# The low parts of the xBC weights are formed on GpSimd

## The chip, the core and the metric

The kernel runs on one core of one Trainium2 chip. Its time is the device time of one execution in microseconds (us), the median of several runs. Five engines work beside each other, each through its own queue in order: TensorE (PE: matmuls and transposes), VectorE (DVE), ScalarE (ACT), GpSimd (POOL) and SyncE (SP), which issues nearly all DMAs.

## The reference

One decoder layer on 1024 tokens of width 1024. What matters here is the mixer: one input projection gives q, k, v, a gate z, xBC and dt. Group A is attention with a window of 128 over 8 heads, group B a state-space scan in chunks of 128:

```
h = rmsnorm(x, norm1) * (1 + scale1) + shift1
proj = h @ w_in                              # -> q | k | v | z | xBC | dt
y_attn = rmsnorm(sliding_window_attention(q, k, v, sinks, rel_bias))
xbc = silu(conv4(xBC) + conv_b)              # depthwise, 1024 channels -> xs, B, C
y_ssm = rmsnorm((ssd_scan(xs, dt, A, B, C) + D_skip * xs) * silu(z))
x = x + gate1 * (concat(y_attn, y_ssm) @ w_o)
x = x + gate2 * swiglu(rmsnorm(x, norm2) * (1 + scale2) + shift2)
out = rmsnorm(x, final_norm)
```

All in float32.

## The kernel before

Every large product is made of three matmuls on split operands: a high part, rounded to the format fp32r, and a low part, the rest. `mm3` (L93 to L96) adds high x high (L94), high x low (L95) and low x high (L96). A weight tile is split by `split`: ScalarE casts the raw tile to the high part (L90), VectorE subtracts it from the raw tile (L81, called from L91). `load_w` (L205) takes a raw buffer from a ring of three, loads it by a DMA on SP's queue and splits it into one of three slots for high and low parts. A raw buffer is free once both its cast and its subtraction have read it; SP issues its DMAs in program order, so a load that waits for a buffer also holds what is behind it.

The stages around the change: q and k projections, then v, z and dt (`vz_tile`), then from about 156 us attention tiles 0 to 3 (`attn`), the xBC projection and convolution of the first half of the sequence (`xbc_tile(0, f)`, f = 0 to 7), between them rows of the modulation weights through the same raw ring (`ada_row`, L409 on VectorE), scan chunks 0 to 3 (`ssd_chunk`), attention tiles 4 to 7 and `xbc_tile(1, f)`; then the output projection from 316 us, the second norm at 394 us, the scan chunks 4 to 7 beside the first SwiGLU columns, and SwiGLU up to the end.

`xbc_tile` multiplies one 1024 x 128 tile of weights by 512 tokens: 24 matmuls into the bank psx. Three of the 16 tiles are loaded ahead (`xw`); the other 13 call `load_w` here (L503). ScalarE copies the bank (L508) and makes the first conv step (L513), VectorE the other three (L515), then ScalarE a tanh (L517) and VectorE the product (L518).

The chain of an attention tile: scores on TensorE (pss, L459), bias and maximum on VectorE (L463, eight), a small subtraction (L81, 128x8), exponentials on ScalarE (L467, L469), transposes on TensorE (pst, L479), copies on ScalarE, the product with v (psy, L486), scaling on VectorE (L84), squares on ScalarE (L490), one column on VectorE (L145), its power on GpSimd (L146), scaling on ScalarE (L492), transposes on TensorE (psm_a, L438). That of a scan chunk: seg (L581), decay on ScalarE, cb and its causal product (L591), three products on VectorE (L84), the skip product on GpSimd (L603), the state's decay on GpSimd (L625), ydg and st on TensorE (L613, L621), sums on VectorE (L87), squares on ScalarE (L629), L145, the power L146, scaling (L632), transposes (psm_s, L438).

The order of instructions on each engine is laid down when the program is built, by a scheduler that places every instruction by its own estimate of when its inputs will be ready; each engine then keeps that order on the chip.

Of the kernel before, what the change touches and what calls it, by code (L numbers as in the profile page):

```python
# [7 lines left out]
F32 = mybir.dt.float32  # L8
F32R = mybir.dt.float32r
AF = mybir.ActivationFunctionType  # L10
ALU = mybir.AluOpType
# [4 lines left out]
P = 128  # L16
D = 1024
KT = 8
# [20 lines left out]
def hymba_layer(ctx: ExitStack, tc: tile.TileContext, x, ada01, ada_rest, w_qk, w_vz, w_xbc,  # L39
                w_o, w_gu, w_dn, prm, bc, rel, adab_g, fnorm, cst, out):  # L40
    nc = tc.nc
# [29 lines left out]
    def dma(out, in_):  # L71
        tc.keep_in_program_order(nc.sync.dma_start(out, in_))

    def mm_bank(name):
        return PS.tile([P, 512], F32, tag="mm", bufs=4, name=name)
# [4 lines left out]
    def sub(out, a, b):  # L80
        nc.vector.tensor_tensor(out=out, in0=a, in1=b, op=ALU.subtract)  # L81
# [7 lines left out]
    def split(h, l, raw):  # L89
        nc.scalar.copy(h, raw)  # L90
        sub(l, raw, h.bitcast(F32))  # L91
# [102 lines left out]
    def wtiles(shape):  # L194
        n = 1
        for d in shape:
            n *= d
        raw = raw_ring(shape)
        hl = ws_ring([2, n])
        h, l = hl[:, 0], hl[:, 1]  # L200
        if len(shape) == 2:
            h, l = (v.rearrange("p (a b) -> p a b", a=shape[0]) for v in (h, l))
        return raw, h, l

    def load_w(src, shape):  # L205
        raw, h, l = wtiles(shape)
        dma(raw, src)
        split(h, l, raw)
        return h, l

    def ada_load(sec, kt, ring_):
# [131 lines left out]
    for kt in range(KT):  # L343
        raw = raw_ring([648])
        dma(raw, w_vz[kt])
        w2 = view(WV, 1296 / 256 * (kt - 3), [2, 648]) if kt >= 3 else view(FR, 64 + 5.0625 * kt, [2, 648])
        h, l = w2[:, 0], w2[:, 1]
# [25 lines left out]
    def fm_tile(half, h, l, bank, kts=range(KT)):  # L373
        for kt in kts:
            mm3(bank, h[:, kt], l[:, kt], hts[half][kt][:, 0], hts[half][kt][:, 1], kt == 0, kt == KT - 1)
# [45 lines left out]
    dma(brow, adab_g[0:1])  # L421
    add(arow[0:1], arow[0:1], brow)
    xw = [load_w(w_xbc[f], [KT, P]) for f in range(3)]
    for t in range(4, 8):
        vz_tile(t)
# [74 lines left out]
              [view(FA, 56.03125 + 2 * f, [512]) for f in range(4)] + [view(FA, 46, [512]), view(FB, 18, [512]), view(FB, 20, [512]), view(FA, 64.03125, [512])]]  # L500

    def xbc_tile(half, f):
        h, l = xw[f] if half == 0 and f < len(xw) else load_w(w_xbc[f], [KT, P])  # L503
        ps = mm_bank(f"psx{half}_{f}")
        fm_tile(half, h, l, ps)
        rw = xraw_ring([515])
        nc.vector.tensor_copy(rw[:, 0:3], halo[:, f])
        nc.scalar.copy(rw[:, 3:515], ps)  # L508
        if half == 0:
            nc.vector.tensor_copy(halo[:, f], rw[:, 512:515])  # L510
        y = xbc_sb[half][f]
        cw = lambda k: pt[:, C_CW + 8 * k + f:C_CW + 8 * k + f + 1]
        nc.scalar.activation(y, ps, AF.Identity, scale=cw(3), bias=pt[:, C_CB + f:C_CB + f + 1])  # L513
        for k in range(3):
            nc.vector.scalar_tensor_tensor(out=y, in0=rw[:, k:k + 512], scalar=cw(k), in1=y, op0=ALU.mult, op1=ALU.add)  # L515
        th = th_ring([512])
        nc.scalar.activation(th, y, AF.Tanh, scale=0.5)  # L517
        nc.vector.scalar_tensor_tensor(out=y, in0=th, scalar=1.0, in1=y, op0=ALU.add, op1=ALU.mult)  # L518
# [133 lines left out]
    for f in range(8):  # L652
        xbc_tile(0, f)
        for _ in range(MOD_ROWS[f]):
            sec, kk = rows.pop(0)
            ada_row(sec, [view(FB, 18, [D])] if sec == 3 else mod2[1], [kk])
# [6 lines left out]
    for f in range(8):  # L663
        xbc_tile(1, f)
# [60 lines left out]
    def gate_up(f, half, out, then=None):  # L725
        pss = []
        for s in range(2):
            if (f, s) not in resident:
                resident[(f, s)] = load_w(w_gu[f + NF * s], [KT, P])
            h, l = resident[(f, s)]  # L730
            ps = mm_bank(f"psgu{f}{s}{half}")
            for kt in range(KT):
                t = h2[half][kt]
                mm3(ps, h[:, kt], l[:, kt], t[:, 0], t[:, 1], kt == 0, kt == KT - 1)
            pss.append(ps)
            if then:
                then(s)
        nc.scalar.activation(out, pss[0], AF.Silu)
        mul(out, out, pss[1])
# [182 lines left out]
    for i in range(NP):  # L922
        a = pair_ring([4, 512])
        for r in range(2):
            f = 2 * i + r
# [230 lines left out]
```

## Time and profile before

| | |
|---|---|
| median of 3 runs | 1148.93 us (1146.12 to 1150.82) |
| the profiled execution | 1144.76 us, span 1143.0 us |
| PE busy | 1105.0 us, 97% of the span |
| DVE busy | 842.6 us, 74% |
| ACT busy | 517.2 us, 45% |
| POOL busy | 244.6 us, 21%, 185 instructions |

Busy shares are means over stages with different limits, so the stretch around the change is read by itself. PE's busy time is modelled at the end of each matmul. Spans on POOL are rough. A row's last part in square brackets is the idle time of the engine ahead of it and what ended that.

### The profile page before, as it was taken

How to read it: one execution, taken by the hardware profiler on the slowest of the kernel's cores; microseconds unless marked ns; L12 is line 12 of the kernel's file. 1: busy time of each engine (PE TensorE's matmuls, PEld its weight loads, DVE VectorE, ACT ScalarE, POOL GpSimd, SP SyncE). 2: the span in 40 equal slices, each digit the busy share in tenths (PEclk: the TensorE clock that was granted, in tenths of full speed). 3: DMA queues.
4: the chain of work that ended last, by engine and by line, in shares of the span. 5: the costliest groups of instructions: out<-in, count | busy, mean ns of one | idle time of the engine just before them, and what ended most of it. 6: DMA issues, size and time to landing. Idle time of an engine off the chain costs nothing. (4 is left out here: it accounts for less than half of the span.)

```text
span 1143.0 us, 15497 instructions
## 1 busy us (share of the span) xinstructions
PE 1105.0 (97%) x5376; PEld 912.4 (80%) x5376; DVE 842.6 (74%) x1490; ACT 517.2 (45%) x1007; POOL 244.6 (21%) x185
## 2 busy tenths in 40 slices
PE   7999999999999889999999999999999999999996
PEld 6788987787788668887888888888888878888875
DVE  6895368788856466546888888898788648787856
ACT  4573256756565456535443333333333325555431
POOL 0100000001200111000222124554445010451352
PEclk9999999999999969999999999999999999999998
DMA  7555644421320253236753247556764468788733
GB/s 267 189 173 174 238 151 145 137 74 38 148 75 19 102 185 119 76 127 221 249 189 125 67 148 263 194 179 217 256 201 160 157 226 306 252 292 281 234 104 147
DMA packets 80449, 197.29 MB, mean 173 GB/s; under 512 B 9154, under 2 KB 10226, under 8 KB 80244
## 3 DMA queue, kind: packets, MB, share of 16 engines
q1 hardware_dynamic: 74164, 184.95, 47.4%
q10 hardware_dynamic: 6208, 11.37, 2.8%
q8 instruction: 42, 0.69, 0.2%
q14 instruction: 35, 0.29, 0.1%
HBM read 149.87 MB, written 47.98 MB: 173 GB/s over the span
## 5 line engine op out<-in xcount | busy, mean ns | idle before, releaser
L81 DVE TENSOR_TENSOR FR<-FP,FR 128x512 fp32r<-128x512 f32 (+4 forms) x244 | 195.0, 822 | 68.8 <-ACT FR L90 68.3
L90 ACT CAST FR<-FP 128x512 fp32r<-128x512 f32 (+3 forms) x236 | 157.7, 682 | 185.6 <-PE psg L95 79.8
L797 POOL TENSOR_TENSOR GF<-GF 128x512 f32<-128x512 f32 x77 | 124.0, 1633 | 68.9 <-DMA GF<-in_w_dn 65.8
L94 PE MATMUL psg<-FR 128*128 128x512 f32 x306 | 119.0, 389 | 0.0
L95 PE MATMUL psg<-FR 128*128 128x512 f32 x306 | 119.0, 389 | 0.0
L96 PE MATMUL psg<-FR 128*128 128x512 f32 x306 | 119.0, 389 | 0.0
L146 POOL TENSOR_TENSOR FP<-FP 128x1 f32<-128x1 f32 (+1 forms) x40 | 28.3, 713 | 407.8 <-DVE FP L145 351.6
L87 DVE TENSOR_TENSOR GF<-GF,psg 128x512 f32<-128x512 f32 x126 | 84.2, 680 | 30.4 <-PE psg L96 27.9
L90 ACT CAST FR<-GF 128x512 fp32r<-128x512 f32 x77 | 47.4, 619 | 79.8 <-PE psg L95 54.5
L94 PE MATMUL psg<-GR,FR 128*128 128x512 f32 x198 | 77.0, 389 | 0.0
L95 PE MATMUL psg<-GR,FR 128*128 128x512 f32 x198 | 77.0, 389 | 0.0
L96 PE MATMUL psg<-GR,FR 128*128 128x512 f32 x198 | 77.0, 389 | 0.0
L81 DVE TENSOR_TENSOR FR<-GF,FR 128x512 fp32r<-128x512 f32 x77 | 73.1, 951 | 0.9 <-ACT FR L90 0.7
L95 PEld LDWEIGHTS psg<-FR 128*128 128x128 f32 x306 | 57.4, 188 | 12.0
L94 PEld LDWEIGHTS psg<-FR 128*128 128x128 f32 x306 | 57.4, 188 | 11.9
L96 PEld LDWEIGHTS psg<-FR 128*128 128x128 f32 x306 | 57.4, 188 | 11.9
L803 POOL TENSOR_TENSOR GD<-GD 128x512 f32<-128x512 f32 x23 | 35.7, 1562 | 119.7 <-ACT GD L415 57.7
L800 POOL TENSOR_TENSOR GF<-GF 128x512 f32<-128x512 f32 x11 | 15.5, 1405 | 194.3 <-DVE GF L84 156.2
L94 PE MATMUL psgu<-FR 128*128 128x512 f32 x128 | 51.6, 407 | 2.5 <-DVE FR L179 1.3
L94 PE MATMUL psx<-FR 128*128 128x512 f32 x128 | 52.2, 408 | 0.0
L96 PE MATMUL psgu<-FR 128*128 128x512 f32 x128 | 51.4, 403 | 0.5 <-DVE FR L81 0.5
L95 PE MATMUL psx<-FR 128*128 128x512 f32 x128 | 51.8, 405 | 0.0
(318 smaller groups left out, 2748.6 us busy)
## 6 DMA issues: line engine op xcount, KB each, us to landing
FP<-in_w_gu SPq DMA_DIRECT2D x52, 512.0 KB, 4.2
FP<-in_ada_rest SPq DMA_DIRECT2D x24, 512.0 KB, 4.4
actds<-GF SPq DMA_DIRECT2D x44, 256.0 KB, 2.7
GF<-in_w_dn SPq DMA_DIRECT2D x22, 512.0 KB, 4.6
wdndt<-GF SPq DMA_DIRECT2D x44, 256.0 KB, 4.4
FP<-actds SPq DMA_DIRECT2D x44, 256.0 KB, 4.4
FP<-wdndt SPq DMA_DIRECT2D x44, 256.0 KB, 4.4
FP<-actda SPq DMA_DIRECT2D x33, 256.0 KB, 4.2
```

The costliest lines, as they stand in the source:

```text
L81: nc.vector.tensor_tensor(out=out, in0=a, in1=b, op=ALU.subtract)
L87: nc.vector.tensor_tensor(out=out, in0=a, in1=b, op=ALU.add)
L90: nc.scalar.copy(h, raw)
L94: nc.tensor.matmul(ps, lhsT=lh, rhs=rh, start=first, stop=False)
L95: nc.tensor.matmul(ps, lhsT=lh, rhs=rl, start=False, stop=False)
L96: nc.tensor.matmul(ps, lhsT=ll, rhs=rh, start=False, stop=last)
L146: nc.gpsimd.tensor_tensor(out=r, in0=r, in1=mhalf[:, 0:count], op=ALU.pow)
L797: nc.gpsimd.tensor_tensor(out=out, in0=a, in1=b, op=ALU.subtract)
L800: nc.gpsimd.tensor_tensor(out=out, in0=a, in1=b, op=ALU.add)
L803: nc.gpsimd.tensor_tensor(out=out, in0=a, in1=b, op=ALU.mult)
```

## The change

`load_w` gets a parameter for the engine that forms the low part; without it VectorE does, as before. The 13 calls from `xbc_tile` name GpSimd. The cast stays on ScalarE. Lines behind `load_w` move down by one, and in the changed kernel the cast and subtraction of `load_w` are L208 and L209.

```
-    def load_w(src, shape):
+    def load_w(src, shape, low=None):
         raw, h, l = wtiles(shape)
         dma(raw, src)
-        split(h, l, raw)
+        nc.scalar.copy(h, raw)
+        (low or nc.vector).tensor_tensor(out=l, in0=raw, in1=h.bitcast(F32), op=ALU.subtract)
         return h, l
...
     def xbc_tile(half, f):
-        h, l = xw[f] if half == 0 and f < len(xw) else load_w(w_xbc[f], [KT, P])
+        h, l = xw[f] if half == 0 and f < len(xw) else load_w(w_xbc[f], [KT, P], nc.gpsimd)
```

The scheduler then lays the engines out anew from the fourth xBC tile to the middle of the first output projection; SP's order is the same.

GpSimd, from the norms of the first stage to scan chunk 1, before (L146 128x1 are powers of row norms, the last four of the twelve those of attention tiles 0 to 3):

```order
L146 TENSOR_TENSOR FP<-FP 128x1 x12
L603 TENSOR_TENSOR FB<-FB,FP 128x512
L146 TENSOR_TENSOR FP<-FP 128x2
L625 TENSOR_TENSOR FA<-FA,FP 128x512
L603 TENSOR_TENSOR FB<-FB,FP 128x512
L146 TENSOR_TENSOR FP<-FP 128x2
```

And now, in the changed kernel's line numbers:

```order
L146 TENSOR_TENSOR FP<-FP 128x1 x9
L209 TENSOR_TENSOR FR<-FP,FR 128x1024
L146 TENSOR_TENSOR FP<-FP 128x1
L209 TENSOR_TENSOR FR<-FP,FR 128x1024 x3
L146 TENSOR_TENSOR FP<-FP 128x1
L209 TENSOR_TENSOR FR<-FP,FR 128x1024 x2
L146 TENSOR_TENSOR FP<-FP 128x1
L209 TENSOR_TENSOR FR<-FP,FR 128x1024 x3
L604 TENSOR_TENSOR FB<-FB,FP 128x512
L146 TENSOR_TENSOR FP<-FP 128x2
L209 TENSOR_TENSOR FR<-FP,FR 128x1024
L626 TENSOR_TENSOR FA<-FA,FP 128x512
```

Nine of the thirteen stand between the powers of attention tile 0 and scan chunk 0; the powers of tiles 2 and 3 come behind three and two of them.

ScalarE, at the end of attention tile 1 (FR<-psm_a is the cast of its transposed output, FR<-FP 128x1024 a weight cast, L469 or L470 the exponentials of tile 2), before:

```order
L492 ACTIVATE FA<-FA,FP 128x512
L90 CAST FR<-FP 128x1024
L440 CAST FR<-psm_a_1557 128x4x128
L508 COPY FA<-psx_3_1860 128x512
L467 ACTIVATE FP<-FP 128x8
L469 ACTIVATE FB,FP<-FB,FP 128x256 x8
```

And now:

```order
L493 ACTIVATE FA<-FA,FP 128x512
L208 CAST FR<-FP 128x1024
L441 CAST FR<-psm_a_1557 128x4x128
L208 CAST FR<-FP 128x1024
L468 ACTIVATE FP<-FP 128x8
L470 ACTIVATE FB,FP<-FB,FP 128x256 x8
```

A second weight cast, the third of the thirteen, stands ahead of the exponentials, where the copy of a finished xBC bank stood; that copy is now behind them.

TensorE, at scan chunk 0 (psx_0_2709 and psx_1_2745 are the banks of xBC tiles 0 and 1 of the second half, with 24 matmuls each), before, where 19 of tile 1 are done:

```order
L96 MATMUL psx_1_2745<-FR 128x512
L94 MATMUL psx_1_2745<-FR 128x512
L581 MATMUL seg_0_2120<-FR 128x512
L581 MATMUL seg_1_2124<-FR 128x512
L587 MATMUL cb_2128<-FA 128x128 x2
```

And now:

```order
L96 MATMUL psx_0_2709<-FR 128x512
L94 MATMUL psx_1_2745<-FR 128x512
L95 MATMUL psx_1_2745<-FR 128x512
L96 MATMUL psx_1_2745<-FR 128x512
L94 MATMUL psx_1_2745<-FR 128x512
L95 MATMUL psx_1_2745<-FR 128x512
L96 MATMUL psx_1_2745<-FR 128x512
L582 MATMUL seg_0_2120<-FR 128x512
L582 MATMUL seg_1_2124<-FR 128x512
L588 MATMUL cb_2128<-FA 128x128 x2
```

Chunk 0 begins 13 matmuls earlier, after 6 of tile 1.

## Rows read from the trace of the kernel before

**Rows 1.** Windows: us, busy us (count) of PE, PEld, DVE, ACT, POOL; PEclk; DMA

```profile
156.00:236.00 80.00, 74.68 (x425) 60.27 (x423) 67.00 (x181) 54.20 (x132) 4.90 (x4) 1.00 0.45 149
236.00:316.00 80.00, 77.09 (x414) 62.23 (x413) 68.82 (x120) 46.53 (x93) 13.04 (x11) 1.00 0.25 86
316.00:394.00 78.00, 77.36 (x454) 63.41 (x452) 43.81 (x124) 45.26 (x129) 2.21 (x4) 1.00 0.14 46
394.00:420.00 26.00, 18.68 (x72) 13.89 (x73) 19.07 (x41) 12.63 (x21) 5.56 (x6) 0.66 0.57 208
```

**Rows 2.** Waits of PE, 156 to 316 us: total us, times, longest us

```profile
PE psm_a L438 <- ACT FA L492: 3.4, 4, 1.1
PE psm_s L438 <- ACT FA L632: 2.0, 3, 1.0
PE pst L479 <- ACT FB L469: 1.1, 2, 0.8
```

**Rows 3.** Lines by form, DVE, 156 to 316 us: busy us, mean ns

```profile
L81 DVE TENSOR_TENSOR FR<-FP,FR 128x1024 fp32r<-128x1024 f32 x13 | 15.8, 1214 | 0.5 <-ACT FR L90 0.5
```

**Rows 4.** Source lines L797 and L146, POOL: ns minimum/median/maximum, first and last start

```profile
L797 POOL TENSOR_TENSOR GF<-GF x77: 1275/1734/2175, 561.9 to 923.5; 128x512 f32<-128x512 f32 x77
L146 POOL TENSOR_TENSOR FP<-FP x40: 544/556/1461, 10.8 to 1137.9; 128x1 f32<-128x1 f32 x32, 128x2 f32<-128x2 f32 x8
```

**Rows 5.** Timeline of POOL and DVE near 562 us: start us, us

```profile
561.92 5.57 POOL L797 TENSOR_TENSOR GF<-GF 128x512 f32<-128x512 f32 x3
...
562.85 1.79 DVE L81 TENSOR_TENSOR FR<-GF,FR 128x512 fp32r<-128x512 f32 x1
```

**Rows 6.** Timeline of PE, ACT and DVE at attention tile 1, 175 to 178 us

```profile
175.67 0.39 PE L94 MATMUL psx<-FR 128*128 128x512 f32 x1
...
177.03 0.39 PE L94 MATMUL psx<-FR 128*128 128x512 f32 x1
...
177.94 0.44 PE L479 MATMUL pst<-FP,FB 128*128 128x128 f32 x2 [0.30 <-ACT FB L469]
...
175.09 1.05 ACT L90 CAST FR<-FP 128x1024 fp32r<-128x1024 f32 x1 [1.04 <-DMA FP<-in_w_xbc]
...
175.98 0.69 DVE L518 SCALAR_TENSOR_TENSOR FA<-FA 128x512 f32<-128x512 f32 x1
176.59 0.16 DVE L81 TENSOR_TENSOR FP<-FP 128x8 f32<-128x8 f32 x1
```

**Rows 7.** Timeline of DVE and SP before attention tile 2, 196 to 198 us

```profile
196.55 1.22 DVE L81 TENSOR_TENSOR FR<-FP,FR 128x1024 fp32r<-128x1024 f32 x1
...
197.83 0.33 SPq L72 DMA_DIRECT2D FP<-in_w_xbc  x1
```

**Rows 8.** DMA issues, 150 to 320 us: count, KB each, median us to landing

```profile
FP<-in_w_xbc SPq DMA_DIRECT2D x13, 512.0 KB, 3.8
```

**Rows 9.** Timeline of ACT, DVE and POOL at attention tile 2, 204 to 210 us

```profile
204.62 1.05 ACT L90 CAST FR<-FP 128x1024 fp32r<-128x1024 f32 x1
...
208.06 1.21 DVE L81 TENSOR_TENSOR FR<-FP,FR 128x1024 fp32r<-128x1024 f32 x1
...
208.22 1.46 POOL L146 TENSOR_TENSOR FP<-FP 128x1 f32<-128x1 f32 x1 [18.89 <-DVE FP L145]
```

**Rows 10.** Timeline of DVE at scan chunks 0 and 1, 243 to 278 us

```profile
243.55 1.21 DVE L81 TENSOR_TENSOR FR<-FP,FR 128x1024 fp32r<-128x1024 f32 x1
...
246.63 1.22 DVE L81 TENSOR_TENSOR FR<-FP,FR 128x1024 fp32r<-128x1024 f32 x1 [0.54 <-ACT FR L90]
...
248.69 1.22 DVE L84 TENSOR_TENSOR FR<-FB,FP 128x1024 fp32r<-128x1024 f32 x1
...
259.64 1.21 DVE L81 TENSOR_TENSOR FR<-FP,FR 128x1024 fp32r<-128x1024 f32 x1
...
275.58 1.22 DVE L81 TENSOR_TENSOR FR<-FP,FR 128x1024 fp32r<-128x1024 f32 x1
...
276.79 1.22 DVE L81 TENSOR_TENSOR FR<-FP,FR 128x1024 fp32r<-128x1024 f32 x1
```

## The prediction

> **What bounds the kernel now.** I read the windows first, then TensorE's waits, then the engines around each wait. The 13 moved subtractions all run between 156 and 316 us, while the two half-sequence xBC convolutions, attention tiles 0 to 3 and scan chunks 0 to 3 are interleaved. In that stretch TensorE is busy 74.68 and 77.09 us of 80 and 80 [rows 1], so 160 - 151.8 = 8.2 us are open. VectorE is busy 67.00 + 68.82 = 135.8 of 160 us (85%), ScalarE less, GpSimd 17.9 us. So TensorE's matmuls bound the stretch, and its 8.2 us of gaps come from chains on the other engines. The waits name them [rows 2]: 3.4 us before the transposes of the attention output (psm_a), 2.0 us before those of the scan output (psm_s), 1.1 us before those of the probabilities (pst). After the stretch TensorE hardly waits (77.36 of 78 us [rows 1]), so a gap made or closed in the stretch stays in the total. 8.2 us is 0.7% of the run: no relief of VectorE there can give more.
>
> **What is removed.** Thirteen instructions on VectorE of 1.214 us each, 15.8 us [rows 3].
>
> **What is added.** Thirteen subtractions of 128x1024 on GpSimd. The trace has none of that size. The nearest is the 128x512 tensor_tensor with two full SBUF inputs, 1.275 us at its shortest, 1.734 us median, 2.175 us longest; a one-column one takes 0.544 us [rows 4]. If the whole 0.544 is a fixed part, a 128x1024 takes 2 x (1.275 - 0.544) + 0.544 = 2.0 us; if nothing is fixed, 2.55 us; with contention on both halves 4.35 us. Whether a write in the rounded format (fp32r) costs GpSimd anything extra no row shows; on VectorE it does not. I take 2.4 us, near the end without a fixed part, since that row has the same operands: 13 x 2.4 = 31 us.
>
> **What GpSimd does to VectorE.** Near 562 us GpSimd runs three 128x512 in a row in 5.57 us, and VectorE's 128x512 subtraction beside them takes 1.79 us [rows 5]; a two-input 128x512 with GpSimd at rest takes 0.69 us [rows 6]. The two alternate: one runs, the other waits. It goes both ways: a one-column power on GpSimd beside one of the moved subtractions takes 1.46 us and not its usual 0.556 [rows 4, 9]. [...] How much of the 31 is felt depends on what stands next on VectorE, so I went through the places.
>
> **First attention tile, at 176 us.** The cast of the first moved tile ends at 176.14 (175.09 + 1.05); VectorE then runs a 0.69 us instruction from 175.98, and behind it stands the small subtraction that all exponentials wait for, at 176.59 [rows 6]. ScalarE's and VectorE's order here is unchanged. In the alternation seen above GpSimd's subtraction gets its turn at 176.6 and holds it until 179.0, and the small one, with two SBUF inputs, comes behind it: 2.4 us later. TensorE's wait before pst at 177.94 (now 0.30 us) grows to about 2.7. The matmul order up to here is the same in both kernels, so nothing covers it: +2.4 us. If the small one gets in first, 0.
>
> **Second tile, at 190 to 198 us.** The third cast now stands on ScalarE ahead of the exponentials. Its data cannot be there at once: SP issues that weight load only when the subtraction of the tile before frees its buffer, at 197.83 just behind 196.55 + 1.22 [rows 7]. On GpSimd that subtraction would follow its cast at 191.0 and free the buffer at 193.4; with a landing of 3.8 us [rows 8] ScalarE's queue stands until 197.2 and the exponentials begin near 198.4, some 0.9 us later than now. But TensorE's new order has 17 xBC matmuls between the scores and pst where 13 stood. One matmul comes each (177.03 - 175.67) / 6 = 0.227 us [rows 6], so four are 0.9 us: 0 in sum. The weights themselves come earlier, not later (193.4 against 197.8 us), so no matmul waits for them.
>
> **Powers behind subtractions.** GpSimd now has subtractions right ahead of the powers of tiles 2 and 3. The cast ends at 205.67 (204.62 + 1.05), a 2.4 us subtraction after at most 0.7 us of contention ends near 208.1 to 208.8, and a free power of 0.55 ends at 208.7 to 209.3; now it ends at 208.22 + 1.46 = 209.7, disturbed by the very subtraction that moves [rows 9]. Cost 0 or a little gain; the wait of TensorE behind it (the longest psm_a wait, 1.1 us [rows 2]) stays: 0.
>
> **Scan chunks.** TensorE's new order brings chunk 0 forward: seg0 comes after 6 matmuls of xBC tile 1 of the second half instead of after 19, that is 13 x 0.227 = 2.95 us earlier, and psm_s0 to psm_s3 stand 11 to 13 matmuls earlier likewise, while psm_a of attention tiles 2 and 3 stands 5 later. So this order only pays if the chain really comes about 3 us sooner. Between 243 and 250 us VectorE loses two subtractions (1.21 + 1.22 us) ahead of the product that seg0 needs at 248.69, ready at 249.91 [rows 10]; with one conv step moved behind it the product comes some 3 us earlier, as planned. [...] At the end of chunk 0 the subtraction at 259.64 leaves the chain, which the new order has already spent. In chunks 1 and 2 a subtraction stands on GpSimd ahead of the skip product (L603), costing that about 3 us, while VectorE loses subtractions just ahead of L145 (in chunk 1 those at 275.58 and 276.79 [rows 10]): 0 each, give or take 1.5. Sum of the scan: +1.5 us, between -3 (no lock felt) and +7.
>
> **Sum.** 2.4 + 0 + 0 + 1.5 = 3.9, say +4 us. On the profiled execution (span 1143.0, time 1144.76) that is 1149 us. The median of the runs shown, 1148.93, lies 4.2 us above that execution, so against it I say 1153 us, 0.35% more. A measurement of this kernel tells no less than about 0.5% (5.7 us) from no change, so this is "no change", leaning to slower.
>
> **Rivals.**
> [...]
> Port bound. Every subtraction holds VectorE for its whole 2.4 us: 13 x (2.4 - 1.214) = 15.4 us more, VectorE at 135.8 + 15.4 = 151 of 160 us. With 24 us idle now on VectorE a third of it is absorbed, and TensorE waits some 10 us more: 1159 us. It decides once instructions with two inputs beside the subtractions take 3 us, above all in the scan, where L84, L515 and L87 follow each other. For it: in that stretch most of VectorE's large instructions have two SBUF inputs. [...] The same comes out if the fp32r write makes the subtraction 4 us. [...]
> [...]
>
> **How the numbers follow.** Forecast (+1 to +7 us) 0.55, own range 1150 to 1156; relief 0.20, most of it between -1 and -5.7; port bound 0.20; clock 0.05. Faster by over 0.5% takes the far end of relief and part of the clock: 0.07. Slower by over 0.5% takes port bound, the upper part of the forecast's size and part of the clock: 0.36. Within 0.5%: 0.57. The range leaves out the far ends: 1145 to 1162 us.
>
> **What would show it.** Right: GpSimd rows of 128x1024 at 2.0 to 2.6 us; the pst wait near 178 us above 2 us; the small L81 (128x8) there at 2 us or more; TensorE's open time in the stretch at 10 to 15 us instead of 8.2. Wrong: subtractions of 4 us or more; psm_s waits gone and the stretch shorter; a clock below 1.00 inside it.

## The result, and the profile after

The changed kernel takes 1163.4 us (median of 4 runs, 1162.5 to 1165.0) against 1147.5 us before (4 runs here): ratio 1.0137, 95% interval 1.0116 to 1.0157. It is 1.4% slower, above the range of the forecast. The profiled execution took 1162.51 us, span 1160.7.

The loss lies in one place. From the first xBC matmul to the first matmul of the output projection (the stretch, from here on) the kernel before took 158.9 us, the changed one 175.1 us, 16.2 us more; from there to the end the two differ by 2 us. The windows over this stretch (columns as in [rows 1]), of before:

```profile
156.40:315.30 158.90, 150.68 (x830) 121.61 (x829) 134.71 (x294) 99.64 (x224) 17.94 (x15) 1.00 0.35 118
```

and of the changed kernel:

```profile
156.10:331.20 175.10, 157.20 (x832) 127.15 (x831) 138.52 (x286) 100.43 (x226) 50.90 (x28) 0.95 0.32 107
```

Two things are to be read here. The length less PE's busy time is 8.2 us before and 17.9 us now: TensorE waits 9.7 us more. And the same matmuls (830 and 832 records) are busy for 157.2 us instead of 150.7: 6.5 us more, at a mean granted clock of 0.95 instead of 1.00. 9.7 + 6.5 = 16.2. VectorE's busy time has grown too, from 134.7 to 138.5 us, though 15.8 us of subtractions left it.

The waits of PE in the stretch, which answer to [rows 2]:

```profile
PE psm_a L439 <- ACT FA L493: 5.7, 4, 2.2
PE psm_s L439 <- ACT FA L633: 4.5, 2, 3.6
PE seg L582 <- DVE FR L84: 3.5, 1, 3.5
PE pst L480 <- ACT FB L470: 2.4, 2, 2.0
PE psc L546 <- DVE FP L644: 1.1, 1, 1.1
```

Where no wait was above 1.1 us there are now five between 2.0 and 3.6 us: before pst of attention tile 1, psm_a of tiles 2 and 3, seg of chunk 0 and psm_s of chunk 2.

GpSimd's and VectorE's lines in the stretch, by form; the first answers to the estimate of 2.4 us, the others to [rows 3, 4]:

```profile
L209 POOL TENSOR_TENSOR FR<-FP,FR 128x1024 fp32r<-128x1024 f32 x13 | 33.6, 2588 | 48.6 <-ACT FR L208 45.1 <-PE pss L460 3.5
...
L516 DVE SCALAR_TENSOR_TENSOR FA<-FA,FP 128x512 f32<-128x512 f32 x39 | 37.1, 950 | 1.6 <-ACT FA L514 1.4
...
L511 DVE COPY FP<-FA 128x3 f32<-128x3 f32 x8 | 4.5, 566 | 0.2 <-ACT FA L509 0.2
```

The subtraction on GpSimd takes 2.59 us in the mean, what VectorE's instructions beside it cost included (2.35 us at its shortest). The conv step L516, 0.777 us in the mean before, takes 0.950, and the copy of three columns L511, 0.162 us before, takes 0.566.

Attention tile 1 (timeline; answers to [rows 6]):

```profile
174.33 1.06 ACT L208 CAST FR<-FP 128x1024 fp32r<-128x1024 f32 x1 [0.97 <-DMA FP<-in_w_xbc]
...
175.29 0.69 DVE L519 SCALAR_TENSOR_TENSOR FA<-FA 128x512 f32<-128x512 f32 x1
175.89 2.33 DVE L81 TENSOR_TENSOR FP<-FP 128x8 f32<-128x8 f32 x1
...
175.46 2.74 POOL L209 TENSOR_TENSOR FR<-FP,FR 128x1024 fp32r<-128x1024 f32 x1 [6.14 <-ACT FR L208]
...
179.01 0.44 PE L480 MATMUL pst<-FP,FB 128*128 128x128 f32 x2 [2.04 <-ACT FB L470]
```

The subtraction comes behind the L519 of VectorE, the small subtraction comes behind it and ends at 178.22 with it, and pst waits 2.04 us instead of 0.30.

Attention tiles 2 and 3 (timeline; answers to [rows 9]):

```profile
209.24 1.05 ACT L208 CAST FR<-FP 128x1024 fp32r<-128x1024 f32 x1 [1.10 <-DMA FP<-in_w_xbc]
...
211.00 0.15 DVE L145 TENSOR_SCALAR FP<-FP 128x1 f32<-128x1 f32 x1
...
210.42 2.90 POOL L209 TENSOR_TENSOR FR<-FP,FR 128x1024 fp32r<-128x1024 f32 x1 [6.97 <-ACT FR L208]
213.29 1.00 POOL L146 TENSOR_TENSOR FP<-FP 128x1 f32<-128x1 f32 x1
...
215.10 0.66 PE L439 MATMUL psm_a<-FP,FA 128*128 128x128 f32 x4 [2.18 <-ACT FA L493]
...
230.99 1.95 DVE L511 COPY FP<-FA 128x3 f32<-128x3 f32 x1
...
230.51 2.40 POOL L209 TENSOR_TENSOR FR<-FP,FR 128x1024 fp32r<-128x1024 f32 x1 [10.35 <-ACT FR L208]
```

In tile 2 the column that the power needs is there at 211.15; the power starts at 213.29, when the subtraction ahead of it in GpSimd's queue is done. In tile 3 a copy of three columns, with one input, stands for 1.95 us beside a subtraction, with the conv steps and L145 behind it.

Chunks 0 and 2 (timeline; answers to [rows 10]):

```profile
252.46 2.50 DVE L563 TENSOR_SCALAR FB<-FB,FP 128x128 f32<-128x128 f32 x1
255.00 1.23 DVE L84 TENSOR_TENSOR FR<-FB,FP 128x1024 fp32r<-128x1024 f32 x1
...
252.53 2.35 POOL L209 TENSOR_TENSOR FR<-FP,FR 128x1024 fp32r<-128x1024 f32 x1 [5.57 <-ACT FR L208]
...
256.37 1.19 PE L582 MATMUL seg<-FR 32*128 32x512 f32 x2 [3.47 <-DVE FR L84]
...
295.61 3.69 DVE L516 SCALAR_TENSOR_TENSOR FA<-FA,FP 128x512 f32<-128x512 f32 x2
...
301.03 1.69 DVE L516 SCALAR_TENSOR_TENSOR FA<-FA,FP 128x512 f32<-128x512 f32 x1
...
294.50 2.80 POOL L209 TENSOR_TENSOR FR<-FP,FR 128x1024 fp32r<-128x1024 f32 x1
...
299.31 2.86 POOL L209 TENSOR_TENSOR FR<-FP,FR 128x1024 fp32r<-128x1024 f32 x1 [0.55 <-ACT FR L208]
```

L563 is the last scaling before the product that seg0 needs. It has one input and takes 0.35 us alone; here it ends with the subtraction, 2.50 us after its start, and TensorE, which the new order has brought to seg0 early, stands for 3.47 us. In chunk 2 three conv steps that should take 2.2 us take 5.4.

The granted clock behind such a wait, in windows around the one before seg0:

```profile
249.00:252.90 3.90, 3.89 (x18) 2.88 (x16) 3.83 (x14) 2.19 (x4) 0.37 (x1) 1.00 0.17 67
252.90:256.40 3.50, 0.03 (x1) 0.06 (x1) 3.46 (x3) 0.66 (x1) 1.98 (x1) 0.86 0.14 16
256.40:262.20 5.80, 5.80 (x18) 4.67 (x19) 3.48 (x6) 3.72 (x7) 0.00 (x0) 0.50 0.21 83
262.20:270.00 7.80, 7.80 (x43) 6.74 (x43) 4.26 (x7) 2.52 (x7) 1.60 (x2) 1.00 0.10 28
```

TensorE is fully busy up to 252.9, idle for 3.5 us, then fully busy for 5.8 us at a granted clock of 0.50, and then at 1.00 again. Such pieces stand behind the waits of pst (3.4 us), seg0 and psm_s2 (6.8 us each): some 17 us at half clock, the end of the wait included, in a stretch that had none before.

### The profile page after: what moved, and what is told of

It reads as the page before. It is cut to its first block, busy times and chain, and to the rows that moved or that the text cites. A ratio compares the mean times of both kernels' runs of the same rounds, so it can differ in the third digit from the quotient of the medians.

```text
span 1160.7 us, 15512 instructions
## 1 busy us (share of the span) xinstructions
PE 1112.1 (96%) x5376; PEld 920.3 (79%) x5376; DVE 848.4 (73%) x1477; ACT 517.0 (45%) x1007; POOL 275.8 (24%) x198
## 4 chain that ended last, share of the span: by engine, by line
PE 57%; DVE 8%; issue 7%; ACT 3%; POOL 3%; DMA 3%; SPq 0%; ACTq 0%; DVEq 0%; POOLq 0%
PE psg L95 10%; PE psg L96 10%; PE psg L94 10%; PE wo L95 2%; PE wo L96 2%; PE wo L94 2%; DVE FR L81 2%; POOL GD L804 1%; PE psgu L96 1%; DVE FA L516 1%; PE psgu L95 1%; PE psgu L94 1%; PE psy L487 1%; DMA h2d<-FA 1%; PE ydg L614 1%
## 5 line engine op out<-in xcount | busy, mean ns | idle before, releaser
L90 ACT CAST FR<-FP 128x512 fp32r<-128x512 f32 (+3 forms) x209 | 129.4, 634 | 156.6 <-PE psg L95 81.9
L81 DVE TENSOR_TENSOR FR<-FP,FR 128x512 fp32r<-128x512 f32 (+4 forms) x217 | 163.2, 776 | 46.6 <-ACT FR L90 45.7
L146 POOL TENSOR_TENSOR FP<-FP 128x1 f32<-128x1 f32 (+1 forms) x40 | 27.0, 681 | 366.0 <-DVE FP L145 304.4
L804 POOL TENSOR_TENSOR GD<-GD 128x512 f32<-128x512 f32 x23 | 33.2, 1455 | 122.5 <-ACT GD L416 57.2
L94 PE MATMUL psx<-FR 128*128 128x512 f32 x128 | 53.3, 416 | 0.0
L94 PE MATMUL psgu<-FR 128*128 128x512 f32 x128 | 51.0, 402 | 2.3 <-DVE FR L179 1.3
L96 PE MATMUL psx<-FR 128*128 128x512 f32 x128 | 52.9, 413 | 0.0
L95 PE MATMUL psx<-FR 128*128 128x512 f32 x128 | 52.7, 412 | 0.0
```

The lines of the kernel that those rows point to most:

```text
L94: nc.tensor.matmul(ps, lhsT=lh, rhs=rh, start=first, stop=False)
L95: nc.tensor.matmul(ps, lhsT=lh, rhs=rl, start=False, stop=False)
L96: nc.tensor.matmul(ps, lhsT=ll, rhs=rh, start=False, stop=last)
L146: nc.gpsimd.tensor_tensor(out=r, in0=r, in1=mhalf[:, 0:count], op=ALU.pow)
L804: nc.gpsimd.tensor_tensor(out=out, in0=a, in1=b, op=ALU.mult)
```

## Experiments

My theory after the result: GpSimd's subtraction and VectorE exclude each other for whole instructions (the lock); the waits that follow grow to 2 to 3.5 us, and behind them the clock falls (to 0.50 behind seg0's). The first rival: the scheduler's new order (scan chunks 11 to 13 matmuls earlier, a weight cast ahead of the exponentials) costs by itself. All numbers of the stretch, from windows like the two above (open is length less PE busy):

| kernel | time to before, 95% interval | stretch us | open us | PE busy us | PEclk |
|---|---|---|---|---|---|
| before | 1 | 158.9 | 8.2 | 150.7 | 1.00 |
| changed | 1.0137 (1.0116 to 1.0157) | 175.1 | 17.9 | 157.2 | 0.95 |
| changed, again | 1.0129 (1.0108 to 1.0150) | 173.7 | 18.1 | 155.6 | 0.96 |
| subtractions left out | 1.0013 (0.9994 to 1.0031) | 156.7 | 5.9 | 150.8 | 0.99 |
| the same, again | 0.9998 (0.9983 to 1.0012) | 156.6 | 6.7 | 149.9 | 1.00 |
| on both engines | 1.0206 (1.0172 to 1.0241) | 181.1 | 20.5 | 160.7 | 0.93 |
| in halves | 1.0140 (1.0106 to 1.0173) | 168.8 | 14.0 | 154.9 | 0.97 |
| zeros written instead | 1.0031 (1.0009 to 1.0053) | 155.1 | 4.7 | 150.5 | 1.00 |
| first half only | 1.0078 (1.0047 to 1.0108) | 161.8 | 10.5 | 151.3 | 1.00 |
| the same, again | 1.0055 (1.0034 to 1.0076) | 161.9 | 10.6 | 151.3 | 1.00 |
| second half only | 1.0106 (1.0066 to 1.0145) | 172.0 | 14.7 | 157.3 | 0.95 |
| waits filled | 1.0245 (1.0198 to 1.0291) | 191.3 | 17.5 | 173.8 | 0.96 |
| copies on ScalarE | 1.0157 (1.0126 to 1.0188) | 174.3 | 18.0 | 156.3 | 0.97 |

### The subtractions left out

```
-        (low or nc.vector).tensor_tensor(out=l, ...)
+        if low is None:
+            nc.vector.tensor_tensor(out=l, ...)
```

> The 13 subtractions of the moved tiles are left out on every engine; their low slots keep older low parts, so the low x high product of those tiles is of other data. The engines' order is close to that of the changed kernel (PE: 76 rows of a listing differ, against 308 from the kernel before). Lock theory (GpSimd's subtractions hold VectorE back for their whole length, and the gaps of 2 to 3.5 us that follow let TensorE's clock fall): without them the gaps and the new half-clock stretches inside 156 to 331 us go, VectorE is 15.8 us lighter than before, 1143 to 1149 us. Order rival (the new order of the matmuls, scan chunks 11 to 13 matmuls earlier, is itself what costs): 1157 us or more, with the waits at psm_a2, psm_a3, seg0 and psm_s2 still above 1.5 us.

The order rival falls. In an order close to the changed kernel's, but without the lock, the stretch takes 156.7 us and the time is that of before. PE's waits:

```profile
PE psm_a L440 <- ACT FA L494: 3.8, 4, 1.9
...
PE psm_s L440 <- ACT FA L634: 0.6, 1, 0.6
```

The waits of seg and psc are gone, psm_s is below [rows 2]. One wait of 1.9 us, psm_a2, remains without any subtraction: a weight cast that waits 3.03 us for its DMA stands on ScalarE ahead of the squares of tile 2, where the new order put it. This one sign of the order rival held. The clock from 156 to 236 us is 0.98, which answers to some 3 us at half clock (0.02 x 80 / 0.50, an estimate); in the repetition it is 1.00 over the stretch. The run also gives the worth of the relief: VectorE has 15.8 us less, and the stretch gains 2.2 us.

### The same once more

> The kernel without the 13 subtractions once more (their low parts hold older data). Its first profile had a stretch from the first xBC matmul to the first of the output projection 2.2 us shorter than before, but 826 us from there to the end, against 819 before, with a wait of 3.06 us for a cast of the down weights at 933 us (before: 1.06). If that later loss was chance of that execution: 818 to 821 us after the stretch, 1142 to 1147 us, a little faster than before. If relief given early is lost again later in this kernel: 824 us or more after the stretch, a wait of 2 us or more near 933 us again, 1147 to 1150 us.

The stretch is again 2.3 us shorter, and the time, 1146.6 us, again that of before. So the relief, small as it is, does not show at the end. The expectation is not decided: the time lies in its first range, but in the profile the last matmul comes 824.2 us after the stretch, as in the second, with a wait of 1.8 us near 933 us. PE's waits from 520 to 1130 us in this kernel:

```profile
PE dna L94 <- ACT FR L90: 1.8, 1, 1.8
PE psgu L94 <- DVE FR L179: 1.5, 3, 1.0
PE dnf L94 <- ACT FR L90: 1.3, 1, 1.3
PE psgu L96 <- DVE FR L81: 1.1, 2, 0.9
```

The kernel before has 1.1, 1.3, 0.9 and 0.5 us in the same places: 1.9 us more are waited for, on split operands in SwiGLU. Behind the stretch this profile is 5.6 us longer than that of before (833.3 against 827.7 us), and what the rest of it is I have not found, nor whether the relief must be lost.

### On both engines

```
+        if low is not None:
+            low.tensor_tensor(out=l, ...)
+        nc.vector.tensor_tensor(out=l, ...)
```

> Each of the 13 low parts is formed twice, first on GpSimd and then once more on VectorE into the same place. The engines' order is close to that of the kernel before (PE: 42 rows differ, against 220 from the changed kernel). Lock theory: the lock is there and VectorE keeps its 15.8 us, so no better than the changed kernel: 1162 to 1172 us. Order rival: the order of before keeps the time of before, 1146 to 1152 us, VectorE having been 85% busy and TensorE the bound.

As the theory said, 1170.3 us. With the matmuls nearly in before's order the lock costs as much as in the new one, and more: the new order is not what the loss needs.

### In halves

```
+            for i in (0, 4):
+                low.tensor_tensor(out=l[:, i:i + 4], in0=raw[:, i:i + 4], ...)
```

> Each GpSimd subtraction of 128x1024 is cut into two of 128x512. Lock theory with the length of one hold deciding: each hold is 1.2 to 1.5 us, VectorE gets in between, no gap of TensorE reaches 2 us, the clock stays up: 1149 to 1155 us. If the sum of the holds decides (some 31 us as before): 1160 to 1166 us, the gaps as in the changed kernel.

The time is that of the changed kernel, so the second expectation fits, but the stretch says more. One hold is shorter, the sum longer:

```profile
L213 POOL TENSOR_TENSOR FR<-FP,FR x26: 1264/1300/1768, 175.5 to 295.7; 128x512 fp32r<-128x512 f32 x26
```

(minimum, median and maximum in ns). The stretch is 6.3 us shorter than the changed kernel's: pst waits 1.0 us, seg0 0.4 us, and the mean clock is 0.97 instead of 0.95. psm_a2 (2.0 us) and psm_s2 (3.6 us) stay. At psm_s2 the two halves of one subtraction hold two instructions of the same chain in turn, the product at 294.46 and the conv step at 296.16, for 1.78 us each: a hold cut in two is not gone where the chain's next instruction meets the second half. What the stretch gained was lost behind it, nearly 7 us; why so much I have not found.

### Zeros written instead

```
-        (low or nc.vector).tensor_tensor(out=l, ...)
+            low.memset(l.bitcast(F32), 0.0)
```

> In place of each of the 13 subtractions GpSimd writes zeros over the low part (128x1024, nothing read), so the low x high product of those tiles is zero. Lock theory, with the lock taken for reading: VectorE's two-input instructions are not held back, the small ones beside it take what they take alone, 1143 to 1150 us. [...]

```profile
L212 POOL MEMSET FR<- x13: 951/953/957, 164.7 to 282.7; 128x1024 f32 x13
...
207.40 0.95 POOL L212 MEMSET FR<- 128x1024 f32 x1 [9.94 <-PE psx L96]
207.93 0.45 DVE L514 COPY FP<-FA 128x3 f32<-128x3 f32 x1 [0.18 <-ACT FA L512]
...
242.71 0.95 POOL L212 MEMSET FR<- 128x1024 f32 x1 [7.15 <-PE psx L96]
242.77 1.23 DVE L84 TENSOR_TENSOR FR<-FB,FP 128x1024 fp32r<-128x1024 f32 x1
```

All 13 take the same 0.95 us, whatever VectorE does beside them, and the stretch is the shortest of all; the time is 0.3% above before, less than 0.5% and so no difference here. These GpSimd instructions, of the same size but reading nothing, cost the stretch nothing (155.1 us against 158.9). They are 0.4 as long, and they need not wait for the weights, so the time alone would not prove that it is the reading. The rows say more. The product L84, with two SBUF inputs, takes its usual 1.23 us beside a memset. A copy of three columns does not escape: the one at 207.93 took 0.45 us instead of 0.16 and ended with the memset. So in this trace an instruction that only writes did not hold a two-input product and still held a copy, against the expectation that the small ones would take what they take alone.

### One half at a time

```
-load_w(w_xbc[f], [KT, P], nc.gpsimd)
+load_w(w_xbc[f], [KT, P], nc.gpsimd if half == 0 else None)
```

> Only the 5 tiles of the first half are formed on GpSimd, the 8 of the second half on VectorE. In the changed kernel the first matmul of the second half is 6.0 us late, the last one 15.4 us. Lock theory: the gaps of pst, psm_a2 and psm_a3 stay (2 us each), those of seg0 and psm_s2 are below 1.5 us; +5 to +7 us, 1151 to 1155 us. Order rival: this kernel's matmuls stand as before (78 rows of a listing differ, 218 from the changed kernel), so 1146 to 1149 us.

> The kernel with the first half's 5 tiles on GpSimd once more, with more executions: its profile put only 2.9 us of its loss between the first xBC matmul and the first of the output projection, and 4.3 us ahead of the first xBC matmul, where nothing was changed. If those 4.3 us are chance: 1148 to 1152 us, +0.2 to +0.5%. If they belong to the kernel: 1153 to 1156 us, again with a first xBC matmul near 160.7 us.

> Only the 8 tiles of the second half are formed on GpSimd. Lock theory: pst and psm_a2 wait as before (0.3 and 1.1 us), a gap of 2.5 us or more before seg0 or one of psm_s1 to psm_s3 stays with its half-clock stretch; +8 to +11 us, 1154 to 1159 us. Order rival: the matmuls stand nearly as in the changed kernel (38 rows differ), so 1160 to 1164 us. If the two halves' losses don't add (one wait swallows the other), this and the kernel with the first half alone come out with a sum far from 16 us.

In the stretch the first half's 5 tiles cost 2.9 us (161.8 and 161.9 against 158.9), the second half's 8 tiles 13.1 us (172.0). The sum, 16.0, is nearly the 16.2 of the whole change. The time of the second half's kernel, 1157.6 us, is in the range of the lock theory. The first half has waits of 2.1 us (pst) and 2.2 us (psm_a2) at a clock of 1.00, so its loss is open time alone. The second half has those of psm_a3, seg0 and psm_s2 (2.0, 3.3 and 3.6 us), at a mean clock of 0.95:

```profile
PE psm_a L439 <- ACT FA L493: 4.6, 4, 2.0
PE psm_s L439 <- ACT FA L633: 4.5, 2, 3.6
PE seg L582 <- DVE FR L84: 3.3, 1, 3.3
```

The times of the first half's kernel, 1154.2 and 1153.8 us, lie in the lock theory's range, but 7.0 and 6.2 us above before, more than these 2.9 us. In both profiles TensorE also waits 2.2 and 2.6 us near 57 us, where VectorE waits for a DMA (in_ada) and where the instructions of both kernels are the same; my expectation that this was chance missed, and what brings it I have not found.

### The waits filled

```
+    def fill(ps, a, n=8):
+        for _ in range(n):
+            nc.tensor.matmul(ps[:, 0:P], lhsT=a, rhs=a, start=True, stop=True)
...
+        if name in ("a2", "a3"):
+            fill(ps, view(FB, 14, [P]))
...
+            if t == 0 and j == 0:
+                fill(ps, vt, 30)
```

> The changed kernel, with matmuls that nobody reads put on TensorE ahead of four of its waits: 8 of 128x128 before psm_a2, psm_a3 and psm_s2, 30 of 128x128 in the rounded format before seg0, in the bank that the next real matmul overwrites. Clock part of the lock theory (the half-clock stretches at 255 and 307 us follow from the gaps of 3.5 us and cost 0.4 us each us): those stretches go, the last xBC matmul comes 3 to 6 us earlier than at 330.5 us, 1157 to 1161 us. Rival (the half clock is only a sign of the waits and costs nothing by itself): no earlier, or up to 2 us later by the fillers, 1162 to 1166 us.

1172.4 us, slower than both expectations, and no test of either. The added matmuls changed the order, the fillers took longer than the waits (30 of them stand from 256.4 to 261 us), and the stretch has nearly as much open time as that of the changed kernel and 124 more matmul records, the fillers and real ones that moved in. What the half clock costs is therefore taken from the table: wherever PEclk is 1.00, PE is busy for 149.9 to 151.3 us, and at a lower one for 154.9 and 156.3 (0.97), 155.6 (0.96), 157.2 and 157.3 (0.95) and 160.7 us (0.93), in the same matmuls; only the kernel without subtractions, at 0.99, shows no more.

### Single forms beside a subtraction

```
+    for form, n in ((copy3, 100), (scal128, 60), (sum512, 24), ...):
+        for beside in (False, True):
+            keep(nc.scalar.copy(raw, xin))
+            if beside:
+                for _ in range(4):
+                    keep(nc.gpsimd.tensor_tensor(out=lo, in0=raw, in1=hi.bitcast(F32), op=ALU.subtract))
+            for _ in range(n if beside else 4):
+                keep(form())
```

> Not the layer: the output is a copy of x's first rows. Eight forms of VectorE instruction, one form at a time, first alone, then beside four GpSimd subtractions of 128x1024 back to back, which read the same tile. Lock theory as the forecast had it (only an instruction with two SBUF inputs is held): the conv step (128x512, two inputs) reaches 2 us and more; COPY 128x3 and 128x512, the scaling 128x128, the sum 128x512 and the instructions with a PSUM input and one SBUF input stay at their time alone within 0.2 us. Wider lock, which the changed kernel's trace suggests (COPY 128x3 at 1.6 and 1.95 us, scaling 128x128 at 2.50 us): the copies and the scaling from SBUF reach 1.5 us and more as well; the sum, the score instruction (PSUM and SBUF) and the scaling from PSUM don't.

One row for each form, from the views of single lines: minimum, median and maximum in ns, over those alone and those beside a subtraction:

```profile
L61 DVE COPY dst<-raw x104: 168/169/2206, 6.0 to 36.2; 128x3 f32<-128x3 f32 x104
...
L67 DVE TENSOR_SCALAR dst<-raw x64: 345/347/2383, 37.5 to 70.8; 128x128 f32<-128x128 f32 x64
...
L64 DVE COPY dst<-raw x44: 426/427/2446, 94.8 to 123.9; 128x512 f32<-128x512 f32 x44
...
L77 DVE SCALAR_TENSOR_TENSOR dst<-raw,dst x20: 750/752/2711, 125.5 to 149.4; 128x512 f32<-128x512 f32 x20
...
L80 DVE TENSOR_REDUCE acc<-raw x28: 685/686/687, 72.4 to 92.9; 128x4 f32<-128x512 f32 x28
...
L73 DVE CUSTOM_DVE_ANT_0 dst<-pbank,raw x28: 482/484/485, 151.3 to 166.7; 128x256 f32<-128x256 f32 x28
...
L83 DVE TENSOR_TENSOR dst<-pbank,raw x20: 690/691/692, 168.4 to 183.3; 128x512 f32<-128x512 f32 x20
...
L70 DVE TENSOR_SCALAR dst<-pbank,raw x52: 349/351/352, 185.2 to 206.0; 128x128 f32<-128x128 f32 x52
```

The picture is sharp. The longest conv step is 1.96 us longer than the median, and the longest copy of 128x3, copy of 128x512 and scaling of 128x128 are so by 2.02 to 2.04 us, though these have one input; the subtraction beside them takes 2.35 us. The sum over 128x512 from SBUF, and everything with an input in PSUM (score, addition, scaling), does not feel it: minimum and maximum differ by at most 3 ns. The wider lock is shown.

### The copies on ScalarE

```
-        nc.vector.tensor_copy(rw[:, 0:3], halo[:, f])
+        nc.scalar.copy(rw[:, 0:3], halo[:, f])
...
-        nc.vector.tensor_scalar(out=z, in0=z, scalar1=sel[2], scalar2=sel[3], op0=ALU.mult, op1=ALU.add)
+        nc.scalar.activation(z, z, AF.Identity, scale=sel[2], bias=sel[3])
```

> The changed kernel with the one-input instructions that were seen held (the two COPY 128x3 of each xBC tile, the two last scalings of the scan's preparation) put on ScalarE. Wider lock theory: seg0's wait falls from 3.5 us to below 2, psm_a3's from 2.1 to below 1.5, and what stands next on VectorE (conv steps with two inputs, one-column scalings) is held in their place: 1156 to 1162 us. If only those two instructions carried the loss: 1150 to 1154 us.

```profile
PE psm_s L439 <- ACT FA L633: 5.6, 3, 3.6
...
PE seg L582 <- DVE FR L84: 0.7, 1, 0.7
```

seg0's wait falls from 3.5 to 0.7 us as expected (psm_a3's from 2.1 to 1.4), but the open time of the stretch stays at 18.0 us: the other waits, above all psm_s, ydg and st, grow by as much. The scaling L145 of two columns, 0.166 us before this edit, is now held instead:

```profile
L145 DVE TENSOR_SCALAR FP<-FP 128x2 f32<-128x2 f32 x4 | 2.0, 504 | 2.4 <-ACT FB L630 2.4
```

The time, 1165.5 us, is no better, and above both expectations. Here a hold that one instruction escaped fell on others.

### The changed kernel again

> The changed kernel itself once more, beside the two others on one chip: 1162 to 1165 us, half-clock stretches behind the waits of 2 to 3.6 us again.

The open time is the same to 0.2 us, at 1162.5 us. At the pst wait the clock stays at 1.00 (177 to 183 us), where the changed kernel had 0.51 over 3.4 us; at seg0 and psm_s2 it is 0.53 and 0.52 over 6.8 and 7.0 us. The stretch is 1.4 us shorter with 0.2 us more open time: the same kernel with 3.4 us less at half clock.

## Why the prediction was wrong

**First attention tile** (+2.4 us): right in its mechanism. The pst wait grew by 1.74 us, by the turn-taking that the prediction read from [rows 5], with the small subtraction at 2.33 us.

**Second tile** (0): right. The third cast waits 5.42 us for its DMA on ScalarE, and pst waits 0.31 us instead of 0.82: the four extra matmuls cover it.

**Powers behind subtractions** (0): this step failed. It let the subtraction of tile 2 end near 208.1 to 208.8, about when the column comes. But the whole tile came some 3 us later, the cast ahead of it waited another 1.10 us for its DMA, the subtraction ran from 210.42 to 213.32, and the power, needed from 211.15, stood behind it in GpSimd's queue. In tile 3 another subtraction held a copy ahead of L145. Together psm_a2 and psm_a3 wait 2.44 us more (2.18 + 2.08 against 1.12 + 0.70). For psm_a2 the runs do not part the subtraction from the new order: without subtractions it waits 1.9 us too, behind the cast that waits for its DMA. An order that is right by the schedule's times is no protection where one DMA moves the instruction ahead.

**Scan chunks** (+1.5 us, at most +7): mis-sized. The waits of psc, seg, psm_s and ydg sum to 9.1 us against 2.8, so +6.28 us, near the far end. No run shows the term of 1.5 us that the sum takes for the scan: what the changed kernel showed in its place is a wait of 3.5 us before seg, where none was, 4.5 us instead of 2.0 before psm_s, 1.1 us before psc, and none before ydg (0.8 us before). The prediction reckoned with instructions that have two SBUF inputs. The single forms show one-input ones held too: copies and scaling from SBUF take up to 2.2 to 2.4 us (0.17 to 0.43 alone), while the sum (0.69 us) and those with an input in PSUM (0.35 to 0.69 us) take no more than alone. It was such a scaling, L563, that made seg0 late: on ScalarE it leaves a wait of 0.7 us instead of 3.5.

**Port bound** (0.20, 1159 us): its mechanism is what happened, with other numbers. VectorE was held not for all of the 33.6 us of subtractions but for about half: its busy time is 138.5 us against 122.2 in the kernel without them, 16.4 us. Yet TensorE's open time grew by 9.7 us, just the 10 us that this rival gave, since the holds fell on instructions that chains waited for. The score instructions (0.480 us as before) were spared; in the scan there are none.

**Clock** (0.05): its chance was far too low. In the changed kernel both waits above 2.5 us have a piece at half clock behind them (seg0, 3.5 us: 0.50 over 5.8 us; psm_s2, 3.6 us: 0.50 over 6.8 us), and in its repetition the clock is low at the same two places (0.53, 0.52). Of the waits near 2 us in the changed kernel that of pst has one (0.51 over 3.4 us), those of psm_a2 and psm_a3 (2.2 and 2.1 us) have none (1.00). On both engines, in halves, in the second half and with the copies on ScalarE, with longest waits of 3.6 to 4.7 us, the mean clock of the stretch is 0.93 to 0.97; in the kernel before, with zeros and in the first half, where none is above 2.2 us, it is 1.00. That the waits bring it rests on these rows alone, since the run that filled them was no test. It adds 6.5 us, two thirds of the waits' 9.7 us of growth, and a clock below 1.00 in the stretch was one of the prediction's own signs of being wrong. This is the missing term of the sum: the prediction knew a price for a wait (its length) and none for what comes behind.

**Relief** (0.20), that VectorE's 15.8 us shorten TensorE's waits: refuted by the kernels without subtractions. 15.8 us less on VectorE are worth 2.2 us in the stretch and nothing at the end.

So of the 16.2 us: +1.74 at the first tile, +2.44 at the powers, +6.28 in the scan, -0.78 in smaller waits, which is 9.7 of open time, and 6.5 by the clock. No version here beats the kernel before, not even the one without the work.

## What to carry to other kernels

Before work goes to GpSimd, count what stands beside it on VectorE by form: here those with an input in PSUM and the sum went free (at most 3 ns more), while two-input instructions, copies and scalings from SBUF, of three columns too, stood 2.0 us longer (the longest of each of the single forms) beside a GpSimd subtraction of 2.35 us. Then ask what the relief is worth where TensorE is the bound: leaving the work out altogether takes one run and would have answered it. And do not price a long wait of TensorE at its length alone: here the half clock behind the waits cost two thirds more (6.5 us on 9.7).

## What the runs showed of the hardware

- A copy of 128x3 on VectorE, 0.17 us alone, takes 2.2 us beside a GpSimd subtraction of 128x1024, and a copy of 128x512, 0.43 us alone, 2.45: both lose 2.0 us.
- A subtraction of 128x1024 in fp32r takes 2.35 us on GpSimd undisturbed (1.21 on VectorE), one of 128x512 1.26 us at its shortest, writing zeros over 128x1024 0.95 us; the writing held a copy of 128x3 (0.45 us) and not a product with two SBUF inputs (1.23 us beside it, 1.22 in the kernel before).
- GpSimd's instructions take longer as well: the 13 subtractions 2.59 us in the mean against 2.35 undisturbed, and the skip product of chunks 0 to 3 1.46 us (L604) against 1.12 before.
